# PEER gate matrices with half of the scaled one-hots on GpSimd, and early expert activations in three float32r passes

## The chip, the cores and the metric

The kernel runs on one core of one Trainium2 chip. The metric is the device time of one launch in microseconds (us): the median of the runs shown, which for the kernel before is 4733.09 us (4724.08 to 4733.77, three runs).

The engines are named as the profile names them: PE (TensorE) with its weight loads PEld, DVE (VectorE), ACT (ScalarE), POOL (GpSimd), SP (SyncE, which issues most transfers).

## The reference, cut to what matters

Two layers over 512 latent and 256 context tokens of width 1024. Each layer mixes tokens with four branches and then looks up experts (PEER). The change is in the second part alone, which for each block of 128 tokens computes:

```python
q = (xb @ wq).reshape(PEER_BLOCK, PEER_HEADS, 2, PEER_DQ)
s = jnp.einsum('thpk,hpnk->thpn', q, subkeys)
sv, si = lax.top_k(s, PEER_TOPK)
...
fv, fi = lax.top_k(cand, PEER_TOPK)
e = jnp.take_along_axis(cidx, fi, axis=-1)
gate = jax.nn.softmax(fv, axis=-1)
act = jax.nn.gelu(jnp.einsum('thkd,td->thk', tab_u[e], xb))
return jnp.einsum('thk,thkd->td', gate * act, tab_v[e])
```

With 8 heads and 16 chosen of each, a token has 128 pairs (sub-key i, sub-key j) out of 128 x 128 experts, and a gate for each pair. All arithmetic is float32.

## The kernel before, in words

**Dense and sparse blocks.** Most blocks (four in the first layer, three in the second) don't gather their experts. Their gates are written as a dense matrix over all 128 x 128 experts, and then `dense` runs through every expert. The other blocks gather, with indirect transfers on POOL, while `dense` runs.

**`peer_front`** (L1316) makes the modulated tokens and the best 16 sub-keys of every list. The tokens lie transposed in `u2T`, as a rounded float32r part and a remainder. A product of two such pairs is three passes of PE (`mm3`, L112): high by high, high by low, low by high. The pair is made by `split` (L108): ACT rounds, DVE subtracts. In the kernel before, `modulate` (L361) also keeps the plain float32 tokens of the dense blocks, in `uf` (tile `u2`).

**`chosen`** (L1383) picks, for one block, the 16 best pairs of every head and their gates. Nearly all of it is a chain of small DVE instructions. For a dense block it ends in three PE transposes (L1458) and one DVE copy into `pst` (L1459): rows are slots, columns tokens, with i, j and gate as three planes.

**`build_gates`** (L1461) turns a block's `pst` into the dense matrix, four tokens at a time; I call that a step. A step is one-hot matrices `ohA` (slot x i) and `ohB` (slot x j) for four tokens, `ohB` scaled by the gate, then one PE product per token, `ohA`^T `ohB`. `ohA` is one DVE comparison of 4 x 128 columns (L1472). `ohB` has two ways: unscaled by DVE in the same form and then scaled on ACT token by token (L1478), or for the last `bd` tokens of the four in one DVE instruction per token that compares and scales (L1480). `bd` is 0, 0, 1, 2 for the dense blocks in turn (table `BD`). The products are plain float32, which PE runs as two passes each (L1482). ACT copies the four results into `gsb` (L1483), and SP writes that to DRAM. There are 128 steps in the first layer and 96 in the second. Five buffers each of `ohA` and `ohB` (`OHB`) let DVE run ahead.

**`early_pieces`** (L1490) is filling for PE meanwhile: the activations of 21 sub-keys (first layer) and 26 (second), that `dense` then need not compute. A piece is eight products of 128 x 128 weights `eu` with the tokens (512 columns in the first layer, 384 in the second), in plain float32 from `uf`, then a gelu on ACT and a transfer to DRAM. `ahead` (L251) loads the next piece's weights as far as two buffers go.

**The order.** A scheduler fixes the order of every engine before the launch, by priorities. `layer` (L397) traces 33% (second layer 48%) of the piece products ahead of the gates and the next 67% (52%) spread over the steps, by `UP`; a step's share is held behind the last product of that step and gives way to everything by 3000 in priority:

```python
for n, b in enumerate(dense):
    sT = slots[n % 2]
    self.chosen(l, top, b, tp, sT=sT)
    for _ in self.build_gates(n, sT, G, bp, BD[n], n == nd - 1):
        done += UP[l][1] / steps
        with tc.issue_after(self.last.ins), self.later(3000):
            go_on()
```

So there are two stretches in each layer, which the text calls **the front** (from the end of `peer_front` to the first one-hot product; DVE chooses for the first block, PE runs pieces) and **the gate loop** (first to last one-hot product). `dense` begins after it.

Of the kernel before, what the change touches and what calls it, by code (L numbers as in the profile page):

```python
# [9 lines left out]
F = mybir.dt.float32  # L10
# [9 lines left out]
KC = 8  # L20
# [32 lines left out]
BD = (0, 0, 1, 2)  # L53
# [26 lines left out]
# heads and their width, of the groups whose heads go through the packs  # L80
# [4 lines left out]
def early(l):  # L85
    """the sub-keys whose activations come ahead of the gates: some evenly apart, and the last two"""
    n = EARLY[l] - 2
    return [127 - i * (128 - 256 // EARLY[l]) // n for i in range(n, -1, -1)] + [126]


class Body:
# [28 lines left out]
    def transposes(self, ps, srcs):  # L120
        """the 128 x 128 pieces srcs, transposed side by side into a bank"""
# [50 lines left out]
    def later(self, by):  # L172
        """what is traced here gives way to the next instructions"""
# [77 lines left out]
    def ahead(self, pieces, lead=LOADP):  # L251
        """(tag, buffers, load, run) in turn, matmul by matmul; the loads run ahead as far as the buffers go"""
# [12 lines left out]
    def mod_pieces(self, l, g, p, parts, bufs):  # L265
        """512 columns of the modulation of a layer, their weights in some parts"""
# [32 lines left out]
    def cond_rows(self, conds, p, tmp, **kw):  # L299
        """silu of the first conditions, each on all partitions"""  # L300
# [9 lines left out]
    def mod_columns(self, l, row, p, ms, bufs=3, upto=8):  # L310
        """parts of the modulation column by column on DVE, row: the conditions; a step: 128 columns"""
# [31 lines left out]
    def folded(self, l, which):  # L343
        """columns of the modulation; where the tokens come normalised only, the norm's own factor and shift are in them"""
# [16 lines left out]
    def modulate(self, cols, blocks, h_src, uT, tok=None, pool=None, c0=0, keep=None, ks=range(KC)):  # L361
# [1440 lines left out]
```

## Time and profile before

| what | before |
|---|---|
| median of three runs | 4733.09 us (4724.08 to 4733.77) |
| profiled execution, its span | 4714.6 us (the page gives its span alone; the median is 18.5 us above that) |
| PE, PEld busy | 4504.4 us (96%), 3814.3 us (81%) |
| DVE, ACT busy | 3787.0 us (80%), 2058.5 us (44%) |
| POOL busy | 1086.3 us (23%): 768 indirect transfers |
| chain that ended last | PE 69%, DVE 10%, DMA 8%, issue 6%, ACT 5%, POOL 1% |

How to read it: the shares are means over the whole launch. The two fronts and gate loops together are 518 us of the span, and there the engines are loaded in another way than in `dense`, which is most of the rest. A duration in the profile reaches over the start of the next instruction of the same engine, so the price of one instruction in a row of many is the distance between two starts.

### The profile page before, as it was taken

Reading aid. Unit: us, or ns where it says so; the run is one execution under the profiler, and the core shown is the slowest. Engines: PE = TensorE matmul, PEld = TensorE weight load, DVE = VectorE, ACT = ScalarE, POOL = GpSimd, SP = SyncE. Lnnn points to the kernel's source line nnn. Section 1 sums busy time; section 2 is a strip of 40 time slices with the busy share of each in tenths; the row PEclk is TensorE's granted clock in tenths of the full one; section 3 lists DMA queues with packets and bytes.
Section 4 is the critical chain, followed back from the end, with each engine's and each line's share of the span. In section 5 each row is a group of like instructions: output and inputs, shape, how many; then the busy total and the mean of one; then the engine's idle time right before and its main releaser. Section 6 shows DMA issues by size and latency. Waiting matters only on the chain.

```text
span 4714.6 us, 67359 instructions
## 1 busy us (share of the span) xinstructions
PE 4504.4 (96%) x24113; PEld 3814.3 (81%) x24113; DVE 3787.0 (80%) x7649; ACT 2058.5 (44%) x3956; POOL 1086.3 (23%) x772
## 2 busy tenths in 40 slices
PE   8999999999989999999999798898999999999998
PEld 6978888885668888888888697787877788888887
DVE  7857655899979899999999875866698787777777
ACT  4357654225952222222222354665339633333333
POOL 0000000000006555655556300000000043333341
PEclk9999999999999999999999899999999999999999
DMA  7844332523679999999999676543426798888885
GB/s 278 289 143 124 108 98 88 206 72 119 192 228 346 340 343 332 339 348 348 346 345 342 212 281 190 177 142 98 157 86 185 252 345 299 296 305 309 305 299 195
DMA packets 495791, 1120.38 MB, mean 238 GB/s; under 512 B 43312, under 2 KB 244832, under 8 KB 486368
## 3 DMA queue, kind: packets, MB, share of 16 engines
q1 hardware_dynamic: 384864, 713.38, 44.3%
q0 software_dynamic: 110592, 402.70, 23.7%
q8 instruction: 190, 3.11, 0.3%
q14 instruction: 145, 1.19, 0.1%
HBM read 975.14 MB, written 140.80 MB: 237 GB/s over the span
## 4 chain that ended last, share of the span: by engine, by line
PE 69%; DVE 10%; DMA 8%; issue 6%; ACT 5%; POOL 1%; SPq 0%; POOLq 0%; DVEq 0%; ACTq 0%
PE acc L115 5%; PE acc L117 5%; PE acc L116 5%; PE act L117 4%; PE act L116 4%; PE act L115 4%; PE S L1504 4%; PE mm L117 3%; PE mm L116 3%; PE mm L115 3%; PE mm L1482 3%; DMA gu<-peer_v,pe 3%; PE sg L115 3%; PE sg L116 3%; PE sg L117 3%
## 5 line engine op out<-in xcount | busy, mean ns | idle before, releaser
L1663 POOL DMA_INDIRECT gu<-peer_u,pe x384 | 535.0, 1393 | 3023.1 <-ACT dwh L109 1400.0
L1675 POOL DMA_INDIRECT gu<-peer_v,pe x384 | 551.1, 1435 | 534.4 <-PE acc L117 224.9
L115 PE MATMUL act<-u2T,duh 128*128 128x512 f32 (+1 forms) x1672 | 609.3, 364 | 21.3 <-ACT duh L109 19.2
L117 PE MATMUL act<-u2T,dul 128*128 128x512 f32 (+1 forms) x1672 | 609.3, 364 | 1.4 <-DVE dul L110 1.4
L115 PE MATMUL acc<-dvh,dwh 128*128 128x512 f32 x1536 | 600.2, 391 | 10.5 <-ACT dwh L109 10.3
L116 PE MATMUL act<-u2T,duh 128*128 128x512 f32 (+1 forms) x1672 | 608.4, 364 | 0.0
L116 PE MATMUL acc<-dvl,dwh 128*128 128x512 f32 x1536 | 600.1, 391 | 0.0
L1681 DVE SCALAR_TENSOR_TENSOR gy<-gu,gwt,gy 128x1024 f32<-128x1024 f32 x381 | 488.5, 1282 | 115.2 <-DMA gu<-peer_v,pe 111.9
L1666 DVE SCALAR_TENSOR_TENSOR gu<-gu,px 128x1024 f32<-128x1024 f32 x384 | 462.5, 1220 | 112.1 <-DMA gu<-peer_u,pe 111.4
L117 PE MATMUL acc<-dvh,dwl 128*128 128x512 f32 x1536 | 545.7, 391 | 1.6 <-DVE dwl L110 1.4
L109 ACT ACTIVATE dwh<-dw 128x512 fp32r<-128x512 f32 (+1 forms) x256 | 148.2, 579 | 884.3 <-DVE dw L1551 884.1
L109 ACT ACTIVATE dvh<-dv 128x1024 fp32r<-128x1024 f32 x256 | 263.4, 1052 | 310.4 <-PE rot L117 196.8
L115 PEld LDWEIGHTS act<-u2T,duh 128*128 128x128 f32 x1672 | 315.3, 189 | 60.1 <-ACT duh L109 19.9
L109 ACT ACTIVATE duh<-du 128x1024 fp32r<-128x1024 f32 x209 | 220.8, 1056 | 310.1 <-PE act L116 238.0
L115 PEld LDWEIGHTS acc<-dvh,dwh 128*128 128x128 f32 x1536 | 288.6, 188 | 72.3 <-ACT dwh L109 15.1
L116 PEld LDWEIGHTS act<-u2T,duh 128*128 128x128 f32 x1672 | 315.3, 189 | 37.6
L117 PEld LDWEIGHTS act<-u2T,dul 128*128 128x128 f32 x1672 | 314.9, 188 | 38.1 <-DVE dul L110 2.9
L117 PEld LDWEIGHTS acc<-dvh,dwl 128*128 128x128 f32 x1536 | 288.4, 188 | 64.5 <-DVE dwl L110 4.4
L116 PEld LDWEIGHTS acc<-dvl,dwh 128*128 128x128 f32 x1536 | 288.7, 188 | 57.6
L110 DVE TENSOR_TENSOR dvl<-dv,dvh 128x1024 fp32r<-128x1024 f32 x256 | 308.6, 1218 | 13.4 <-ACT dvh L109 13.4
L1482 PEld LDWEIGHTS mm<-ohB,ohA 128*128 128x128 f32 x1792 | 234.4, 194 | 98.4 <-ACT ohB L1478 48.0
L1504 PE MATMUL S<-u,eu 128*128 128x384 f32 (+1 forms) x752 | 310.7, 537 | 2.0 <-ACT ege L1507 1.2
(386 smaller groups left out, 10684.0 us busy)
## 6 DMA issues: line engine op xcount, KB each, us to landing
dv<-peer_v SPq DMA_DIRECT2D x256, 512.0 KB, 6.4
du<-peer_ut SPq DMA_DIRECT2D x209, 512.0 KB, 6.5
G<-gsb SPq DMA_DIRECT2D x26, 2048.0 KB, 9.2
wmodc<-wmodc SPq DMA_DIRECT2D x84, 512.0 KB, 4.7
gw<-wgb SPq DMA_DIRECT2D x128, 256.0 KB, 2.9
Gt<-G SPq DMA_DIRECT2D x31, 1024.0 KB, 9.7
eu<-peer_ut SPq DMA_DIRECT2D x47, 512.0 KB, 3.9
Gt<-G SPq DMA_DIRECT2D x31, 768.0 KB, 7.0
```

The source lines that it names most:

```text
L109: a = self.nc.scalar.activation(hi, src, AF.Copy)
L110: return a, self.nc.vector.tensor_tensor(lo, src, hi, op=OP.subtract)
L115: mm(out, lh, rh, start=first, stop=False)
L116: mm(out, lh, rl, start=False, stop=False)
L117: self.pe = mm(out, ll, rh, start=False, stop=last)
L1482: self.last = nc.tensor.matmul(ps[:, s % 4, :], A[:, s, :], B[:, s, :], start=True, stop=True)
L1504: nc.tensor.matmul(ps[:, :n], U[:, k, :], uf[:, k, :], start=k == 0, stop=k == KC - 1)
L1663: dma = nc.gpsimd.indirect_dma_start(out=t, out_offset=None, in_=I['peer_u'], in_offset=bass.IndirectOffsetOnAxis(ap=e[:, k:k + 1], axis=0))
L1666: nc.vector.scalar_tensor_tensor(t, t, 1.0, x, op0=OP.mult, op1=OP.mult, accum_out=act[:, k:k + 1])
L1675: dma = nc.gpsimd.indirect_dma_start(out=t, out_offset=None, in_=I['peer_v'], in_offset=bass.IndirectOffsetOnAxis(ap=e[:, k:k + 1], axis=0))
L1681: nc.vector.scalar_tensor_tensor(y, t, w[:, k:k + 1], y, op0=OP.mult, op1=OP.add)
```

## The change

Both edits are in the two stretches just named.

1. In `build_gates` the last two tokens of every four get their scaled `ohB` from POOL, one instruction each (compare, then multiply). For the first two DVE still compares (now 2 x 128 columns) and ACT still scales. The table `BD` and the single-token DVE form are gone.
2. In `early_pieces` the weights are split by ACT and DVE into a float32r pair, two buffers of each, and a product is three passes from `u2T`. The plain tokens `uf` are gone, and `modulate` uses a rotating tile in their place.

Comments are also taken out all over the file; the diff below leaves them out, and a line that was only split differently.

```diff
-BD = (0, 0, 1, 2)
...
-    def modulate(self, cols, blocks, h_src, uT, tok=None, pool=None, c0=0, keep=None, ks=range(KC)):
+    def modulate(self, cols, blocks, h_src, uT, tok=None, pool=None, c0=0, ks=range(KC)):
...
-            u = keep[:, k, c0:c0 + n] if keep is not None else pool.tile([128, 512], F, name="uf", bufs=3 if tok else 2)[:, :n]
+            u = pool.tile([128, 512], F, name="uf", bufs=3 if tok else 2)[:, :n]
...
-                uf = tp.tile([128, KC, nd * 128], F, name="u2", bufs=1)
...
-                fill = [self.early_pieces(l, i, uf, tp) for i in range(EARLY[l])]
+                fill = [self.early_pieces(l, i, uT, nd * 128, tp) for i in range(EARLY[l])]
...
-    def build_gates(self, n, sT, G, p, bd, last):
+    def build_gates(self, n, sT, G, p, last):
...
+        on = GT // 2
...
-                for o, c, k in ((A, 0, GT), (B, 1, GT - bd)):
+                for s in range(on, GT):
+                    t = t0 + q + s
+                    nc.gpsimd.tensor_scalar(B[:, s, :], self.iota, sT[:, 1, t:t + 1], sT[:, 2, t:t + 1], op0=OP.is_equal, op1=OP.mult)
+                for o, c, k in ((A, 0, GT), (B, 1, on)):
                     nc.vector.tensor_tensor(o[:, :k], iota[:, :k], sT[:, c, t0 + q:t0 + q + k, None].to_broadcast([128, k, 128]), op=OP.is_equal)
...
-                        if s < GT - bd:
-                            nc.scalar.activation(B[:, s, :], B[:, s, :], AF.Copy, scale=sT[:, 2, t:t + 1])
-                        else:
-                            nc.vector.tensor_scalar(B[:, s, :], self.iota, sT[:, 1, t:t + 1], sT[:, 2, t:t + 1],
-                                                    op0=OP.is_equal, op1=OP.mult)
+                    if s < on:
+                        nc.scalar.activation(B[:, s, :], B[:, s, :], AF.Copy, scale=sT[:, 2, t:t + 1])
...
-            return U
-
-        def run(U):
+            W = [p.tile([128, KC, 128], R, name="eu" + x, bufs=2) for x in "hl"]
+            self.split(*W, U)
+            return W
+
+        def run(W):
...
-                nc.tensor.matmul(ps[:, :n], U[:, k, :], uf[:, k, :], start=k == 0, stop=k == KC - 1)
+                self.mm3(ps[:, :n], (W[0][:, k, :], W[1][:, k, :]), (uT[0][:, k, :n], uT[1][:, k, :n]), k == 0, k == KC - 1)
```

How the order of the engines moves. First DVE, first layer, in the gate loop of the first block; `ohA` and `ohB` are the one-hots, `tm`, `ij`, `t` and `fi` belong to the choosing for the next blocks. Before:

```order
L1472 TENSOR_TENSOR ohA<-c_iota,pst_10138 128x512
L1472 TENSOR_TENSOR ohB<-c_iota,pst_10138 128x512
L1444 TENSOR_SCALAR tm<-a_12860 128x64
L1406 MAX_INDEX fi<-fv,c_13465 128x8
L1404 MATCH_REPLACE c_13471<-fv,cand 128x112
```

Now, with the remainder `eul` of a split between two one-hots of a step:

```order
L1402 MATCH_REPLACE c_13778<-fv,cand 128x112
L1475 TENSOR_TENSOR ohA<-c_iota,pst_10138 128x512
L109 TENSOR_TENSOR eul<-eu,euh 128x1024
L1475 TENSOR_TENSOR ohB<-c_iota,pst_10138 128x256
L1447 COPY ij_13100<-t_13101 128x64
L1442 TENSOR_SCALAR tm<-a_13091 128x64 x4
```

DVE's second one-hot is half as wide, and the order holds 21 instructions `eul` in the first layer (2 far ahead, 7 in the front, 12 behind it) and 26 in the second (2, 12, 12). In the first layer 51 small instructions of the choosing (37 and 14 value loads) that stood ahead of the first copy to `pst` now stand behind it; in the second layer 14.

Second, ACT, first layer, the gate loop; `ege` is a piece's gelu, which waits for the piece's last product, and `euh` the rounding of the weights of the piece after the next, into the buffer that this piece has read. Now:

```order
L1480 ACTIVATE ohB<-ohB,pst_10138 128x128 x2
L1482 ACTIVATE gsb<-mm 128x4x32x4
L108 ACTIVATE euh<-eu 128x1024
L1507 ACT_TABLE_LOAD
L1507 ACTIVATE ege<-S 128x512
```

Before, that place held `ege` alone, and a step had up to four scalings instead of two. So `euh` is placed just where its buffer comes free, with a whole piece on PE between it and its use.

Third, POOL, the whole of it but its first rows, as one piece of the difference:

```order
-L1663 DMA gu<-peer_u,pe_14713 128x1024 x128
...
+L1473 ISA
+L1473 TENSOR_SCALAR ohB<-c_iota,pst_10138 128x128 x64
+L1473 TENSOR_SCALAR ohB<-c_iota,pst_10139 128x128 x64
...
+L1663 DMA gu<-peer_u,pe_15140 128x1024 x128
...
+L1473 TENSOR_SCALAR ohB<-c_iota,pst_33012 128x128 x64
```

POOL computes only in the gate loops (64 instructions a block, 256 and 192 in all), ahead of each layer's gathers.

## Rows read from the trace of the kernel before

**Rows 1.** The page's first line.

```profile
span 4714.6 us, 67359 instructions
```

**Rows 2.** Busy time by stretch: first layer's front, its loop, then second layer's.

```profile
core 0: us, PE busy (x) PEld busy (x) DVE busy (x) ACT busy (x) POOL busy (x), PEclk, DMA share, GB/s
1071.00:1128.50 57.50, 52.24 (x134) 23.57 (x132) 55.99 (x334) 16.91 (x27) 0.00 (x0) 0.98 0.41 133
1128.50:1364.30 235.80, 226.11 (x1262) 162.59 (x1263) 217.58 (x638) 211.26 (x579) 0.00 (x0) 0.98 0.61 177
3485.00:3543.50 58.50, 57.28 (x185) 34.03 (x184) 56.66 (x329) 19.66 (x38) 0.00 (x0) 1.00 0.40 120
3543.50:3709.70 166.20, 162.03 (x1000) 130.92 (x999) 135.28 (x302) 159.23 (x463) 0.00 (x0) 0.99 0.69 203
```

**Rows 3.** The one-hot products by line: first layer, then second, first and last start.

```profile
L1482 PE MATMUL mm<-ohB,ohA x1024: 272/275/582, 1128.5 to 1364.3; 128*128 128x128 f32 x171
...
L1482 PE MATMUL mm<-ohB,ohA x768: 272/275/513, 3543.5 to 3709.7; 128*128 128x128 f32 x192
```

**Rows 4.** Chain of waits (start, length): ACT, then PE binding, first layer; second layer's pieces.

```profile
1227.87 1.17 ACT ohB L1478 x4
...
1267.69 0.86 PE S L1504 x2
1268.55 0.89 PE mm L1482 x8
...
3577.86 1.29 PE S L1504 x4
```

**Rows 5.** Timeline of DVE: start and length; a step of the fourth block.

```profile
1314.22 0.68 DVE L1472 TENSOR_TENSOR ohA<-c_iota,pst 128x512 f32<-128x512 f32 x1
1314.82 0.41 DVE L1472 TENSOR_TENSOR ohB<-c_iota,pst 128x256 f32<-128x256 f32 x1
1315.16 0.59 DVE L1480 TENSOR_SCALAR ohB<-c_iota,pst 128x128 f32<-128x128 f32 x2
1315.67 0.68 DVE L1472 TENSOR_TENSOR ohA<-c_iota,pst 128x512 f32<-128x512 f32 x1
```

**Rows 6.** Timeline of PE in `dense`: float32r passes, 512 and 384 columns.

```profile
1445.83 0.39 PE L115 MATMUL act<-u2T,duh 128*128 128x512 f32 x1
...
1449.91 0.39 PE L115 MATMUL act<-u2T,duh 128*128 128x512 f32 x1
...
3736.86 0.34 PE L115 MATMUL act<-u2T,duh 128*128 128x384 f32 x1
...
3738.97 0.33 PE L115 MATMUL act<-u2T,duh 128*128 128x384 f32 x1
```

**Rows 7.** By line, ns min/median/max: the split of `dense`, a gathered block's product on DVE.

```profile
L109 ACT ACTIVATE duh<-du x209: 1038/1061/1067, 1376.7 to 4664.5; 128x1024 fp32r<-128x1024 f32 x105
...
L110 DVE TENSOR_TENSOR dul<-du,duh x209: 1205/1218/1299, 1377.8 to 4666.3; 128x1024 fp32r<-128x1024 f32 x105
...
L1666 DVE SCALAR_TENSOR_TENSOR gu<-gu,px x384: 1202/1219/1285, 1405.2 to 4198.2; 128x1024 f32<-128x1024 f32 x192
```

**Rows 8.** Timeline at the ends of the fronts: first layer, then second.

```profile
1125.38 0.57 DVE L1459 COPY pst<-mm 128x384 f32<-128x384 f32 x1
...
1128.48 2.08 PE L1482 MATMUL mm<-ohB,ohA 128*128 128x128 f32 x8 [5.26 <-ACT ohB L1478]
...
3533.73 9.94 PE L1504 MATMUL S<-u,eu 128*128 128x384 f32 x30 [1.22 <-ACT ege L1507]
...
3537.72 0.57 DVE L1459 COPY pst<-mm 128x384 f32<-128x384 f32 x1
```

**Rows 9.** Groups of the first gate stretch (busy, mean ns), and one gather on POOL.

```profile
L1478 ACT ACTIVATE ohB<-ohB,pst 128x128 f32<-128x128 f32 x416 | 135.2, 405 | 12.7 <-DVE ohB L1472 12.6
L1480 DVE TENSOR_SCALAR ohB<-c_iota,pst 128x128 f32<-128x128 f32 x96 | 29.9, 339 | 0.0
...
1402.26 0.94 POOL L1663 DMA_INDIRECT gu<-peer_u,pe  x1 [0.30 <-issue]
```

More of the change, by code (lines that the diff above doesn't have):

```diff
@@ L443, in layer @@
                 slots = [tp.tile([128, 4, 128], F, name=f"pst{i}", bufs=1) for i in range(2)]
-                uf = tp.tile([128, KC, nd * 128], F, name="u2", bufs=1)
-                top = self.peer_front(l, blocks, dense, sparse, uT, uf, kp, tp, hp)
+                top = self.peer_front(l, blocks, dense, sparse, uT, kp, tp, hp)
                 self.ge = self.dram.tile([EARLY[l], 128, nd * 128], F, name=f"ge{l}")
                 bp = self.pool(s2, "pb", 2)
-                fill = [self.early_pieces(l, i, uf, tp) for i in range(EARLY[l])]
+                fill = [self.early_pieces(l, i, uT, nd * 128, tp) for i in range(EARLY[l])]
                 if need:
@@ L468, in layer @@
                     self.chosen(l, top, b, tp, sT=sT)
-                    for _ in self.build_gates(n, sT, G, bp, BD[n], n == nd - 1):
+                    for _ in self.build_gates(n, sT, G, bp, n == nd - 1):
                         done += UP[l][1] / steps
@@ L1313, in outproj, with peer_front @@
             pass
-    def peer_front(self, l, blocks, dense, sparse, uT, uf, kp, tp, hp):
+    def peer_front(self, l, blocks, dense, sparse, uT, kp, tp, hp):
         nc, I = self.nc, self.I
@@ L1340, in peer_front @@
                     u, c0 = (uC, 0) if b == LB else (uT, 128 * b)
-                    self.modulate(cols, blocks[b:b + w], self.z, u, self.x2, tmp, c0, uf if b < len(dense) else None)
+                    self.modulate(cols, blocks[b:b + w], self.z, u, self.x2, tmp, c0)
             hp.release()
@@ L1470, in build_gates @@
                 B = p.tile([128, GT, 128], F, name="ohB", bufs=OHB)
-                for o, c, k in ((A, 0, GT), (B, 1, GT - bd)):
+                for s in range(on, GT):
+                    t = t0 + q + s
+                    nc.gpsimd.tensor_scalar(B[:, s, :], self.iota, sT[:, 1, t:t + 1], sT[:, 2, t:t + 1], op0=OP.is_equal, op1=OP.mult)
+                for o, c, k in ((A, 0, GT), (B, 1, on)):
                     nc.vector.tensor_tensor(o[:, :k], iota[:, :k], sT[:, c, t0 + q:t0 + q + k, None].to_broadcast([128, k, 128]), op=OP.is_equal)
-                for q4 in range(0, GT, 4):
-                    ps = self.ps.tile([128, 4, 128], F, name="mm")
-                    for s in range(q4, q4 + 4):
-                        t = t0 + q + s
-                        if s < GT - bd:
-                            nc.scalar.activation(B[:, s, :], B[:, s, :], AF.Copy, scale=sT[:, 2, t:t + 1])
-                        else:
-                            nc.vector.tensor_scalar(B[:, s, :], self.iota, sT[:, 1, t:t + 1], sT[:, 2, t:t + 1],
-                                                    op0=OP.is_equal, op1=OP.mult)
-                        self.last = nc.tensor.matmul(ps[:, s % 4, :], A[:, s, :], B[:, s, :], start=True, stop=True)
-                    nc.scalar.activation(gs[:, :, q + q4:q + q4 + 4, :].rearrange("p b t j -> p t b j"),
-                                         ps.rearrange("p t (b j) -> p t b j", j=JB), AF.Copy)
+                ps = self.ps.tile([128, GT, 128], F, name="mm")
+                for s in range(GT):
+                    t = t0 + q + s
+                    if s < on:
+                        nc.scalar.activation(B[:, s, :], B[:, s, :], AF.Copy, scale=sT[:, 2, t:t + 1])
+                    self.last = nc.tensor.matmul(ps[:, s, :], A[:, s, :], B[:, s, :], start=True, stop=True)
+                nc.scalar.activation(gs[:, :, q:q + GT, :].rearrange("p b t j -> p t b j"),
+                                     ps.rearrange("p t (b j) -> p t b j", j=JB), AF.Copy)
                 yield
@@ L1488, in build_gates, with early_pieces @@
                 nc.sync.dma_start(G[a:z, :, n * 128 + t0:n * 128 + t0 + TG, :].rearrange("b i t j -> i b t j"), gs[:, a:z])
-    def early_pieces(self, l, i, uf, p):
+    def early_pieces(self, l, i, uT, n, p):
         nc = self.nc
         j = early(l)[i]
-        n = uf.shape[2]
         def load():
```

## The prediction

> **What bounds the kernel now.** I read the busy time by stretch first, because the change lives in two stretches of each layer and the shares of the whole launch say little about them. The gate loop runs from the first to the last one-hot product: 1128.5 to 1364.3 in the first layer, 3543.5 to 3709.7 in the second [rows 3], so 236 and 166 us. In the first loop three engines are nearly full at once: PE 226, DVE 218 and ACT 211 of 236 us. In the second PE has 162 and ACT 159 of 166, DVE 135 [rows 2]. The reader should see that relieving one engine alone gains little, and that POOL has nothing to do there. The chain of waits then shows a step where PE binds: 0.89 us of one-hot products and 0.86 us for a piece's product, one behind the other with no gap [rows 4].
>
> The fronts differ. In the first layer DVE is busy for 56.0 of 57.5 us [rows 2], and PE stands idle for 5.26 us before the first one-hot product, which comes 3 us after the copy to `pst` [rows 8]: the choosing on DVE sets the end. In the second the copy is done at 3538.3, yet PE works on pieces until 3543.5 [rows 8]: PE sets it, with DVE some 5 us ahead.
>
> **Prices, part by part.** *Pieces on PE.* A plain float32 product takes 0.86 us at 512 columns and 1.29 / 2 = 0.645 us at 384 [rows 4]. A float32r pass starts every (1449.91 - 1445.83) / 18 = 0.227 us at 512 columns and (3738.97 - 3736.86) / 12 = 0.176 us at 384, 18 and 12 being the passes between [rows 6]. Three passes cost 0.68 and 0.53 us, so a product gains 0.18 and 0.12 us. The loops hold 109 and 114 such products (the passes counted in the trace, halved): PE gains 20 us in the first, 13 us in the second.
>
> *One-hots on DVE.* Starts lie 0.60 us apart behind 512 columns, 0.34 behind 256, and 0.51 / 2 = 0.255 behind a compare-and-scale of one token [rows 5]; for 384 columns I take the middle, 0.47. A step now costs 0.60 + 0.60 = 1.20 us in blocks with `bd` 0, 0.60 + 0.47 + 0.26 = 1.33 with 1, 0.60 + 0.34 + 0.51 = 1.45 with 2. With 64, 32 and 32 steps that is 77 + 43 + 46 = 166 us in the first loop; with 64 and 32, 77 + 43 = 120 us in the second. The new step is 0.60 + 0.34 = 0.94 us: 120 and 90 us. DVE gains 46 and 30 us.
>
> *Splits.* The rounding costs ACT 1.06 us and the remainder costs DVE 1.22 us [rows 7]. By the order 12 of each lie in either loop: 13 us on ACT, 15 us on DVE. ACT loses 160 scalings in each loop (416 less 256, 352 less 192); at 1.17 / 4 = 0.29 us, where the chain runs through four of them [rows 4], that is 47 us. So ACT is down by 34 us in both and can't bind.
>
> *Fronts.* In the first layer 7 splits, 8.5 us, enter ahead of the copy to `pst`, and the order moves 51 small instructions behind it, which at the front's mean of 56.0 / 334 = 0.17 us [rows 2] are 8.6 us. The front keeps its length; the loop's DVE gets the 8.6 us. PE is done with its pieces earlier and only waits longer. In the second layer 12 splits, 14.6 us, enter and 14 instructions, 2.4 us, leave. The copy then comes 12 us later, less the 1.8 us that DVE idles there now [rows 2]: 3548, and the first one-hot product 3 us behind, 3551 instead of 3543.5. **The second front loses 8 us**, although PE has less to do.
>
> *The rest of the loops, without POOL.* DVE in the first: 218 - 166 + 120 + 15 + 9 = 195 us; in the second 135 - 120 + 90 + 15 + 2 = 123 us. PE: 226 - 20 = 206, and 162 - 13 = 149 us. With the slack that PE has now (10 and 4 us) the loops would take 216 and 153 us.
>
> *POOL.* It gets 256 and 192 instructions of a kind that no row shows on it. The nearest rows are the same compare-and-scale on DVE (0.255 us apart, mean length 0.339) and the scaling alone on ACT (mean 0.405); the far end is POOL's own gather, 0.94 us [rows 5, 9]. I take 0.34 us, the length of the very same instruction, and 0.255 to 0.405 as bounds: 87 us (65 to 104) in the first loop, 65 us (49 to 78) in the second. Either way POOL alone is far from binding.
>
> *POOL beside DVE.* What matters is whether POOL's 87 us lie beside DVE's 195 or in turn with them. The lower bound is no cost: a DVE product with two inputs keeps its median of 1219 ns and never exceeds 1285 over all 384 times, while gathers are issued on POOL [rows 7]. The upper bound is full turns, 195 + 87 = 282 us. The row for the lower bound is of an engine that issues transfers; the new instruction streams 128 columns of `iota` from the memory DVE reads, so I give that row little weight and take turns as the likelier. For its price I go between two counts: turns with one-hots and splits alone, 120 + 15 + 87 = 222 us, everything else of DVE beside; and turns with all of DVE, 282. The middle is 252. In the second loop 90 + 15 + 65 = 170 to 123 + 65 = 188, middle 179.
>
> Here the Trainium skill speaks against the change. "SBUF — State Buffer", section "SBUF: two separate sides", says that GpSimd shares one pair of ports with VectorE, that a VectorE instruction with two SBUF inputs and a GpSimd instruction that reads SBUF exclude each other for their whole length, and that the loser waits. The row on gathers shows no such thing, and no run here has GpSimd computing. By the row the sum is 4708, by the rule it is the forecast.
>
> **The sum.** First loop 252 - 236 = +16, second 179 - 166 = +13, second front +8: +37 us. The sum is made on an execution with a span of 4714.6 us [rows 1], 18.5 below the median; I add it to the median: 4733 + 37 = **4770 us**. With 0.255 us the loops are 230 and 163 (middles): -6 - 3 + 8, 4732. With 0.405 they are 269 and 192: +33 + 26 + 8, 4800; and with 0.405 and full turns 299 and 201: +63 + 35 + 8, 4839.
>
> "GPSIMD Engine Reference", section "Elementwise — side-by-side cycle accounting", gives 769 ns for 512 elements in its best case, an estimate of 0.19 us for 128; no row here shows it. By that price turns would cost so little that PE binds again, and the sum would be 4708.
>
> **The rivals.**
> *POOL beside DVE (faster).* If the two don't exclude each other, PE binds: 216 - 236 = -20, 153 - 166 = -13, +8: -25 us, **4708**. It speaks for it that DVE keeps its pace beside gathers; against it, that DVE is full in the first loop and any loss there shows at once. It decides at a POOL price below about 0.2 us in turns, or at any price below 0.8 us beside (206 / 256).
>
> *The gains cancel (same).* With turns at the low price the sum is 4732. Late splits would do the same to the rival above: each piece's remainder must wait for the last product of the piece two before, then for ACT and for DVE's queue. The order places `euh` where its buffer comes free, a whole piece ahead of its use; eight products with their steps last some 14 us in the loop against 1.06 + 1.22. So I don't expect PE to wait for them. If it did by 1 us in each of 24, 4708 would become 4732.
>
> *POOL alone binds (slower).* At the gather's 0.94 us the loops would be 241 and 180 us even beside DVE: +5 + 14 + 8, 4760. Both ends at once, 0.94 in turns, would be 4733 + 300; I leave that out, since the nearest rows are the same arithmetic.
>
> That the change does not do what it says I exclude: the order shows 64 POOL instructions in each block's place and 21 and 26 splits.
>
> **How the numbers follow.** About 0.2%, 9.5 us, can be told from no change. Turns at 0.34 us or near: 0.48, slower. POOL alone binding: 0.07, slower. Beside, or so short that turns don't matter: 0.33, faster. Cancelled: 0.12, same. So faster 0.33, same 0.12, slower 0.55. The likeliest case's own range is 4745 to 4840. Eight times in ten must reach to the faster case as well: from 4698 (its 4708 without the 10 us of slack that PE has in the first loop) to 4840.
>
> **What would show it.** Right: POOL's instructions stretch where DVE compares, DVE's one-hots lie further apart than 0.60 and 0.34 us or wait, both loops last 250 and 180 us, PE's clock and idle time there get worse, ACT has time to spare, and the second front ends near 3551. Each step alone: product triples at 0.68 and 0.53 us, DVE's remainders at 1.22 us, ACT below 180 us in the first loop. Wrong: loops of 216 and 153 us with PE without gaps (beside), POOL rows in an unbroken line (POOL alone), or PE waiting for `eul` at the start of each piece.

## The result and the profile after

The changed kernel takes **4873.44 us** (median of four runs, 4862.36 to 4879.57); the kernel before, in the four runs beside and before it, takes 4728.59 us. The ratio is 1.0315, with a 95% interval of 1.0302 to 1.0328: slower by 145 us. I had forecast 4770 us, slower, and had given 4840 us as the far end of the range.

The profiled execution of the changed kernel has a span of 4870.1 us, against 4714.6 [rows 1], so 155.5 us are to be found. The table of busy time by stretch, with the columns of [rows 2], for the first front, the first gate loop, the second front and the second loop:

```profile
1078.30:1135.90 57.60, 42.24 (x188) 33.98 (x186) 56.62 (x301) 22.53 (x32) 2.90 (x3) 0.89 0.40 133
1135.90:1437.10 301.20, 242.43 (x1376) 195.56 (x1376) 207.93 (x595) 186.83 (x432) 300.29 (x254) 0.96 0.46 135
3565.60:3633.60 68.00, 56.11 (x313) 54.55 (x311) 65.43 (x324) 29.14 (x43) 2.95 (x3) 0.94 0.40 128
3633.60:3855.00 221.40, 178.62 (x1094) 161.65 (x1095) 133.86 (x302) 139.51 (x321) 221.16 (x190) 0.93 0.48 140
```

The loops last 301.2 and 221.4 us instead of 235.8 and 166.2 [rows 3]: +65.4 and +55.2 us. The reader should look at POOL: it is busy for 300.3 of 301.2 us and for 221.2 of 221.4, while no other engine is full. From the first piece product to the first one-hot product, the first front keeps its 57 us and the second goes from 58.8 to 68.0, +9.2. The modulation ahead of the fronts (first transposition of `z` to first product of the queries) goes from 21.3 to 25.7 us and from 16.1 to 18.6, +4.4 and +2.5. Together that is 137 of the 155.5 us. The rest lies in stretches that the edit does not touch, 10 us of it behind the second loop (from its last one-hot product to the end 1015.1 us against 1004.9, where the runs below show 999 to 1020); the profiled execution of before happens to lie 14 us below the median of its runs, that of after 3 us.

The end of the second front in the timeline, where the copy stood at 3537.72 [rows 8] and the first one-hot product at 3543.5 [rows 3]: the copy comes 92.2 us later than before, 80.9 of it brought along from the stretches ahead of the front, and the first one-hot product now follows the copy by 3.6 us, so that DVE sets the end:

```profile
3629.92 0.56 DVE L1457 COPY pst<-mm 128x384 f32<-128x384 f32 x1
```

```profile
3633.56 2.08 PE L1481 MATMUL mm<-ohB,ohA 128*128 128x128 f32 x8 [5.51 <-ACT ohB L1480]
```

Who waits for whom shows in the view of the line of the one-hot products (durations: minimum, median, maximum in ns; then the idle time of PE and PEld ahead of them, in us and times; then who waited for them):

```profile
L1481 PE MATMUL mm<-ohB,ohA x1792: 270/275/582, 1135.9 to 3855.0; 128*128 128x128 f32 x200
...
  POOL ohB L1473: 229.9, 323
  ACT ohB L1480: 35.1, 27
...
  ACT gsb L1482: 157.8, 166
  DVE ohA L1475: 147.4, 159
```

PE and its weight loads wait for POOL's one-hots, and DVE and ACT wait in turn for PE. The 229.9 us are a sum of two engines that mostly wait side by side: POOL's line, below, has 95.6 us for PE and 134.3 for the weight loads. Behind it stands the line of DVE's compares, after and then before:

```profile
L1473 POOL TENSOR_SCALAR ohB<-c_iota,pst x448: 787/1094/5538, 1133.0 to 3854.0; 128x128 f32<-128x128 f32 x150
...
  PEld mm L1481: 134.3, 173
  PE mm L1481: 95.6, 150
```

```profile
L1475 DVE TENSOR_TENSOR ohA<-c_iota,pst x224: 660/693/864, 1134.4 to 3846.2; 128x512 f32<-128x512 f32 x112
```

```profile
L1472 DVE TENSOR_TENSOR ohA<-c_iota,pst x224: 628/682/762, 1126.6 to 3704.5; 128x512 f32<-128x512 f32 x112
```

One step in the timeline (start and length in us; the last row of POOL is two instructions) puts the two side by side:

```profile
1391.13 0.69 DVE L1475 TENSOR_TENSOR ohA<-c_iota,pst 128x512 f32<-128x512 f32 x1 [1.16 <-PE mm L1481]
1391.31 1.43 POOL L1473 TENSOR_SCALAR ohB<-c_iota,pst 128x128 f32<-128x128 f32 x1
1391.73 0.42 DVE L1475 TENSOR_TENSOR ohB<-c_iota,pst 128x256 f32<-128x256 f32 x1
1392.72 2.21 POOL L1473 TENSOR_SCALAR ohB<-c_iota,pst 128x128 f32<-128x128 f32 x2
1392.79 0.49 PE L1481 MATMUL mm<-ohB,ohA 128*128 128x128 f32 x2 [0.33 <-POOL ohB L1473]
1393.32 0.69 DVE L1475 TENSOR_TENSOR ohA<-c_iota,pst 128x512 f32<-128x512 f32 x1 [1.16 <-PE mm L1481]
```

A step takes 1393.32 - 1391.13 = 2.19 us. DVE compares for 1.03 us of it at the pace it had before, and then idles for 1.16. POOL does one instruction in 1.41 us (1392.72 - 1391.31), beside DVE's compares, and one in 0.78, while DVE idles; then it starts again, without a gap.

Over all steps this is regular. Between POOL instructions that stand back to back the distance of two starts is never below 0.774 us. Where DVE's instructions with two input tiles (the compares, the remainders, and in the choosing the predicated copies) fill under a quarter of that distance, its mean is 0.78 us (168 times); where they fill half to three quarters, 1.28 (134 times); above that, 1.65 (127 times). A straight line through all of them is 0.68 us + 0.63 x (time of DVE's two-input instructions beside it) + 0.10 x (time of DVE's other instructions), which explains 87% of the variance. These times are the recorded lengths, which overlap; cut at the next start, the same fit gives 0.77 instead of 0.63, so 0.63 goes with recorded lengths alone. The mean is 1.179 us, and 256 x 1.179 = 302 us is the first loop.

So there were two theories to try. *Price and turns*: POOL's instruction costs 0.775 us by itself, DVE's two-input work lengthens it to 1.18, POOL alone pays, and POOL thereby binds. *The rest of the change*: splits, remainders and the rotating tile stretch the loops, and POOL only fills the time.

### The profile page after: what moved, and what is told of

The parts are those of the page before. It is cut to its first block, busy times and chain, and to the rows that moved or that the text cites. A ratio compares the mean times of both kernels' runs of the same rounds, so it can differ in the third digit from the quotient of the medians.

```text
span 4870.1 us, 68681 instructions
## 1 busy us (share of the span) xinstructions
PE 4528.4 (93%) x24489; PEld 3911.2 (80%) x24489; DVE 3788.7 (78%) x7568; ACT 2034.9 (42%) x3685; POOL 1611.0 (33%) x1220
## 5 line engine op out<-in xcount | busy, mean ns | idle before, releaser
L1473 POOL TENSOR_SCALAR ohB<-c_iota,pst 128x128 f32<-128x128 f32 x448 | 527.3, 1191 | 2038.7 <-DVE pst L1457 2038.7
L1481 PE MATMUL mm<-ohB,ohA 128*128 128x128 f32 x1792 | 304.1, 300 | 112.5 <-POOL ohB L1473 95.6
L1481 PEld LDWEIGHTS mm<-ohB,ohA 128*128 128x128 f32 x1792 | 260.8, 201 | 171.0 <-POOL ohB L1473 134.3
L116 PEld LDWEIGHTS acc<-dvh,dwl 128*128 128x128 f32 x1536 | 288.6, 188 | 67.8 <-DVE dwl L109 7.7
```

The lines of the kernel that those rows point to most:

```text
L116: self.pe = mm(out, ll, rh, start=False, stop=last)
L1473: nc.gpsimd.tensor_scalar(B[:, s, :], self.iota, sT[:, 1, t:t + 1], sT[:, 2, t:t + 1], op0=OP.is_equal, op1=OP.mult)
L1481: self.last = nc.tensor.matmul(ps[:, s, :], A[:, s, :], B[:, s, :], start=True, stop=True)
```

## The experiments

Loop times are from first to last one-hot product of each run's profile; the ratio is to the kernel before, run beside it on the same chip (medians of 4720 to 4729 us), with its 95% interval. Three kernels were run once and have no interval.

| run | first, second loop | time, us | ratio |
|---|---|---|---|
| before | 235.8, 166.2 | 4728.59 | |
| changed | 301.2, 221.4 | 4873.44 | 1.0315 [1.0302, 1.0328] |
| split pieces alone | 247.0, 173.9 | 4762.64 | 1.0084 [1.0069, 1.0100] |
| POOL half alone | 288.6, 213.2 | 4816.95 | 1.0196 [1.0179, 1.0212] |
| one of four on POOL | 248.1, 169.8 | 4755.92 | 1.0065 [1.0049, 1.0081] |
| one of four, plain pieces | 232.0, 159.5 | 4719.25 | 0.9998 [0.9987, 1.0008] |
| no compares on DVE | 239.9, 165.2 | 4734.77 | one run |
| DVE compares token by token | 269.8, 188.3 | 4794.27 | 1.0147 [1.0122, 1.0172] |
| half of the columns on POOL | 299.5, 211.3 | 4856.08 | one run |
| compare alone on POOL | 255.0, 179.3 | 4775.89 | one run |
| split alone, 8 rotating tiles | 245.9, 172.9 | 4751.51 | 1.0059 [1.0043, 1.0076] |
| remainders on POOL | 251.8, 179.2 | 4778.91 | 1.0125 [1.0108, 1.0141] |
| shared | 251.3, 177.4 | 4774.12 | 1.0111 [1.0092, 1.0130] |
| extra POOL instruction | 249.6, 178.1 | 4772.70 | 1.0110 [1.0093, 1.0127] |

### The two halves of the change

**Split pieces alone**: the changed kernel with `build_gates` and `BD` of before.

```diff
-    for _ in self.build_gates(n, sT, G, bp, n == nd - 1):
+    for _ in self.build_gates(n, sT, G, bp, BD[n], n == nd - 1):
```

> The split pieces alone, the one-hots as before. If POOL's one-hots make the whole loss of the loops (+65 and +55 us), it goes away here: the loops come back to about 240 us (DVE: its 218 of before, 15 of remainders, 9 of work moved out of the front) and 172 us (ACT 159 + 13), no PE wait for a one-hot of over 20 us in all; with the second front's +9 and the rotating tile's +7 the time is 4740 to 4770 us. If the splits or the three passes are what stretches the loops, they stay above 260 and 190 us and the time above 4800.

The loops came out at 247.0 and 173.9 us. The windows of the two loops, columns as in [rows 2]:

```profile
1137.50:1384.50 247.00, 222.37 (x1376) 190.14 (x1376) 239.26 (x691) 224.37 (x592) 0.00 (x0) 0.96 0.56 165
3577.40:3751.30 173.90, 161.04 (x1096) 154.28 (x1096) 154.05 (x334) 172.82 (x481) 0.00 (x0) 0.95 0.61 179
```

DVE binds the first (239 us, 242 by my prices) and ACT the second (173 us, 172 by my prices). The splits are thus a loss of their own, +11 and +8 us in the loops, but not the 65 and 55. The time, 4763, lies in the range that I gave. That PE's waits for a one-hot would be small was wrong: PE and its weight loads together waited 114.2 us for `ohB` as ACT scaled it (PE alone 47.9), where they waited 66.1 (PE 18.1) in the kernel before.

**POOL half alone**: the kernel before with the new `build_gates`.

> Half of the scaled one-hots on POOL alone, the early pieces in plain float32. If POOL binds the loops by itself: PE waits for POOL's one-hots again, by over 150 us in all, the loops are 280 to 300 and 205 to 220 us, the fronts and the modulation are those of before, and the time is 4820 to 4850 us. If the splits on DVE are needed for the loss (DVE too full, POOL shut out by the remainders), the loops are below 260 and 185 us and the time is below 4780.

Loops of 288.6 and 213.2 us, fronts of 56.6 and 58.8 as before; the time, 4817, is 3 us below what I expected. The line of the one-hot products says why (waits of PE and PEld added, as above; PE alone has 60.4):

```profile
  POOL ohB L1475: 161.6, 325
```

POOL's mean distance is 1.128 us here, and 256 x 1.128 = 289. Without the remainders DVE has less two-input work, and POOL is a little shorter: the turns, in small. Against the 4724.25 us of the kernel before in these runs the two halves cost 38 and 93 us, 131 together; both at once cost 145.

### What POOL's instruction costs, and what lengthens it

**No compares on DVE** but one for each block, which leaves most of the first one-hots out of the computation.

```diff
+        A = p.tile([128, GT, 128], F, name="ohA", bufs=1)
+        nc.vector.tensor_tensor(A, iota, sT[:, 0, 0:GT, None].to_broadcast([128, GT, 128]), op=OP.is_equal)
...
-                A = p.tile([128, GT, 128], F, name="ohA", bufs=OHB)
...
-                for o, c, k in ((A, 0, GT), (B, 1, on)):
-                    nc.vector.tensor_tensor(o[:, :k], iota[:, :k], sT[:, c, t0 + q:t0 + q + k, None].to_broadcast([128, k, 128]), op=OP.is_equal)
...
-                        nc.scalar.activation(B[:, s, :], B[:, s, :], AF.Copy, scale=sT[:, 2, t:t + 1])
+                        nc.scalar.activation(B[:, s, :], A[:, s, :], AF.Copy, scale=sT[:, 2, t:t + 1])
```

> DVE's compares of two inputs are taken out of the loop: one product of 128x512 a block, which all its tokens then use as their first one-hot and as the source of the half that ACT scales. This leaves part of the computation out; POOL, PE and ACT issue what they did. If DVE's two-input work is what lengthens POOL's instructions, POOL's rows fall to 0.78 to 0.82 us in the mean and the loops to 205 to 220 and 150 to 160 us (PE binds), time 4715 to 4750 us. If POOL's 1.19 us is its own price beside any busy engine (PE and ACT reading the same memory), the rows stay above 1.1 us and the loops at 290 and 210 us or more.

```profile
L1474 POOL TENSOR_SCALAR ohB<-c_iota,pst x448: 782/788/2381, 1133.0 to 3730.3; 128x128 f32<-128x128 f32 x150
```

The median falls from 1094 to 788 ns, the mean distance to 0.881 us, and the loops to 239.9 and 165.2 us. PE, ACT and the pieces were as busy as before beside it, so it was DVE's work that lengthened POOL's. The mean and the loops miss what I expected (0.82 us and 220, 160). For the mean the reason shows: the remainders and the choosing of the next block are still on DVE, and beside them the distances are 0.88 to 1.24 us. For the first loop it explains a part only: POOL is busy for 224.7 and PE for 221.0 of its 239.9 us, so neither fills it.

**DVE's compares token by token**, with one input tile and a scalar each; ACT scales nothing.

```diff
-                for o, c, k in ((A, 0, GT), (B, 1, on)):
-                    nc.vector.tensor_tensor(o[:, :k], iota[:, :k], sT[:, c, t0 + q:t0 + q + k, None].to_broadcast([128, k, 128]), op=OP.is_equal)
+                for s in range(GT):
+                    t = t0 + q + s
+                    nc.vector.tensor_scalar(A[:, s, :], self.iota, sT[:, 0, t:t + 1], None, op0=OP.is_equal)
+                for s in range(on):
+                    t = t0 + q + s
+                    nc.vector.tensor_scalar(B[:, s, :], self.iota, sT[:, 1, t:t + 1], sT[:, 2, t:t + 1], op0=OP.is_equal, op1=OP.mult)
```

> DVE's six one-hots a step one token at a time, each from one tile and the token's own scalar, instead of two products of two tiles; ACT scales nothing. If only DVE's two-input instructions hold POOL up, POOL's rows fall to 0.78 to 0.90 us; DVE then binds with 6 x 0.255 = 1.53 us a step where it had 0.94: 195 + 75 = 270 us in the first loop and 123 + 57 = 180 in the second, loops 270 to 280 and 180 to 192 us, time 4800 to 4825 us. If any DVE instruction that reads this memory holds POOL up, POOL's rows stay at 1.2 us or above and the loops are 300 and 220 us or longer, time above 4860.

```profile
L1473 POOL TENSOR_SCALAR ohB<-c_iota,pst x448: 783/906/2387, 1130.3 to 3784.2; 128x128 f32<-128x128 f32 x150
```

DVE issues more instructions and is busier (253 of 269.8 us against 208 of 301), and yet POOL's median is 906 ns instead of 1094, and the whole is 79 us faster than the changed kernel. The loops, 269.8 and 188.3 us, have the length that I expected of DVE, and the time is 6 us below; but POOL fills the first as much as DVE does (256 us against 253), and PE and its weight loads wait longer for POOL:

```profile
  POOL ohB L1473: 107.9, 220
  DVE ohB L1479: 25.8, 12
```

So it is not how busy DVE is that lengthens POOL's instructions. What differs is the form of the compares, two input tiles or one; they also became shorter (0.28 us instead of 0.69 at the median), and no run here separates the two.

**Half of the columns.** POOL makes 64 of the 128 columns of its one-hots, DVE the others.

```diff
-                    nc.gpsimd.tensor_scalar(B[:, s, :], self.iota, sT[:, 1, t:t + 1], sT[:, 2, t:t + 1], op0=OP.is_equal, op1=OP.mult)
+                    for e, c in ((nc.gpsimd, 0), (nc.vector, 64)):
+                        e.tensor_scalar(B[:, s, c:c + 64], self.iota[:, c:c + 64], sT[:, 1, t:t + 1], sT[:, 2, t:t + 1],
+                                        op0=OP.is_equal, op1=OP.mult)
```

> POOL makes 64 of the 128 columns of each of its one-hots, DVE the other 64, one token at a time. If POOL's price goes by columns, its shortest start-to-start falls from 0.775 to about 0.39 us; if it is mostly a fixed cost, it stays above 0.6 us. DVE gets 256 more instructions of some 0.2 us, so 195 + 51 = 246 us in the first loop and 123 + 38 = 161 in the second: loops about 250 and 170 us in the first case, 270 or more and 195 or more in the second.

```profile
L1474 POOL TENSOR_SCALAR ohB<-c_iota,pst x448: 570/1200/3216, 1128.8 to 3833.3; 128x64 f32<-128x64 f32 x150
```

The shortest distance is 0.553 us against 0.774: between the two cases. By these two points a fixed 0.33 us and 3.5 ns a column. The median, though, is 1200 ns, longer than for the whole width, and the loops are 299.5 and 211.3 us: DVE got 256 instructions more and is busy for 257 us of the first. What the cheaper POOL instruction gave, the added work of DVE took: POOL is busy for 272 us of that loop, no longer for all of it.

**Compare alone**, without the gate (`op1` and its scalar left out):

> POOL compares and does not multiply by the gate: this leaves the gates of half of the tokens out. If POOL's price is that of its two operations, the shortest start-to-start falls from 0.775 us to 0.5 us or less and the loops to 250 to 270 and 180 to 195 us; if the price is that of streaming 128 columns, whatever is done with them, it stays at 0.70 to 0.78 us and the loops at 295 to 302 and 215 to 222 us.

```profile
L1473 POOL TENSOR_SCALAR ohB<-c_iota,pst x448: 597/1047/4192, 1129.4 to 3761.1; 128x128 f32<-128x128 f32 x150
```

The shortest distance is 0.578 us, so the multiplication costs 0.196 of the 0.774; the loops are 255.0 and 179.3 us. Both operations count, beside a part that is paid once. Here DVE's compares stand beside POOL as in the changed kernel, and a cheaper POOL instruction gives 46 and 42 us back: so POOL's price binds the loops.

### Fewer one-hots on POOL

**One of four**, with split pieces, and **one of four with plain float32 pieces**: `on = 3 * GT // 4` in the changed kernel, and in the run of POOL half alone.

> As changed, but one scaled one-hot of four on POOL instead of two. If POOL's time per instruction (0.78 us alone, 1.2 us beside DVE's compares) is the bound, one a step is 1.2 us against PE's 206 / 128 = 1.6 us a step, and POOL no longer binds: loops 220 to 235 and 155 to 165 us, PE's wait for POOL under 30 us in all, time 4725 to 4745 us. If each POOL instruction takes its time away from DVE whatever their number, DVE has 212 us of its own plus 128 x 0.8 in the first loop and the loops stay at 270 and 190 us or more: time above 4790.

> One scaled one-hot of four on POOL, and the early pieces in plain float32 as before: no splits, no rotating tile, no second front. PE binds with its 226 and 162 us. If POOL's own time is the bound of the change, this is where it costs nothing and DVE and ACT get slack: loops 228 to 234 and 162 to 166 us, time 4715 to 4729 us. If POOL's instructions slow DVE or PE in some other way, the loops are longer than those of before, 245 and 172 or more, and the time is above 4740.

The windows of the loops, first the two with split pieces, then the two with plain ones:

```profile
1134.30:1382.40 248.10, 218.47 (x1369) 190.96 (x1370) 217.38 (x594) 214.92 (x560) 223.61 (x127) 0.94 0.56 164
3583.90:3753.70 169.80, 155.13 (x1094) 149.88 (x1095) 143.38 (x302) 156.45 (x417) 156.95 (x95) 0.96 0.62 183
```

```profile
1127.10:1359.10 232.00, 219.68 (x1255) 162.21 (x1255) 196.55 (x542) 201.71 (x547) 198.75 (x127) 0.97 0.61 180
3540.60:3700.10 159.50, 155.75 (x985) 127.03 (x984) 122.15 (x270) 143.27 (x398) 140.82 (x93) 1.00 0.70 207
```

With split pieces every load is near the one worked out (DVE 217 against 212 us, ACT 215), but the first loop is 248 us, not 220 to 235, and the time 11 us above what I expected: four engines with 215 to 224 us of work each do not run full at once. I read that as a ring of engines that feed one another, which no run tests by itself. POOL alone, with half the instructions, is busy for 224 us; its mean distance is now 1.70 us where instructions stand back to back, I take it because DVE's compares leave it fewer gaps. With plain pieces PE binds again and the loops gain 4 and 7 us. The time is that of the kernel before within the interval: of the gain 6 us are lost behind the second loop (1010.5 us to the end, against 1004.9), inside the scatter of that stretch.

### The smaller terms

**Eight rotating tiles** in the split-only kernel:

```diff
-            u = pool.tile([128, 512], F, name="uf", bufs=3 if tok else 2)[:, :n]
+            u = pool.tile([128, 512], F, name="uf", bufs=8 if tok else 2)[:, :n]
```

> The split pieces alone (the one-hots as before), with eight buffers of the rotating tile of the modulation instead of three. If the three buffers are what lengthens the modulation (23.9 against 19.5 us in the first layer, 18.9 against 16.1 in the second, from the first transposition to the first product of the queries), it comes back to 19.5 and 16.1 and the time falls by 7 us against the split pieces alone: 4750 to 4760 us. If the longer modulation has another cause, both stretches stay and the time is 4758 to 4768 us.

The time fell into the first theory's range, yet its mechanism did not show: from the first transposition of `z` to the first product of the queries it is still 26.7 us in the first layer and 18.6 in the second. (Up to the last transposition, where the expectation's 23.9 and 19.5 us of the first layer end, it is 24.8 us.) The buffers are not the cause. Nor do they make the 11 us in the median (the intervals overlap): between the two profiled executions 5.4 us of it lie ahead of the first modulation and 5.5 between the first loop and the second modulation, where the edit touches nothing. The timeline of DVE in the changed kernel's second modulation shows what else is new there:

```profile
3453.27 1.23 DVE L109 TENSOR_TENSOR eul<-eu,euh 128x1024 fp32r<-128x1024 f32 x1 [1.42 <-ACT euh L108]
3454.41 0.40 DVE L377 TENSOR_SCALAR uf<-mm,fold 128x128 f32<-128x128 f32 x1
3454.73 1.22 DVE L109 TENSOR_TENSOR eul<-eu,euh 128x1024 fp32r<-128x1024 f32 x1
```

The splits of the first two pieces are placed into each layer's modulation: remainders of 2.45 us on DVE, which waits 1.42 us for ACT's rounding ahead of the first. As lengths the remainders match the 2.5 us of the second layer, and leave about 2 of the first layer's 4.4 open. That they alone are the cause is not shown: in the next run, with the remainders on POOL, the second modulation still takes 17.4 us, and DVE there waits 2.21 us for ACT, which rounds the same two pieces.

**Remainders on POOL**, one-hots as before (with the eight tiles), and **shared**: the same, and one one-hot of four on POOL in the first two blocks.

```diff
-            self.split(*W, U)
+            nc.scalar.activation(W[0], U, AF.Copy)
+            nc.gpsimd.tensor_tensor(W[1], U, W[0], op=OP.subtract)
```

> As the last, and the remainders of the split pieces are computed on POOL instead of DVE; no one-hot on POOL. With the price that the runs so far give (0.33 us and 3.5 ns a column) a remainder of 1024 columns takes 3.9 us undisturbed and 4 to 8 us beside DVE's compares, a piece ahead of its use. If POOL pays for the turns and DVE does not: DVE has 227 us in the first loop, ACT 224, loops 228 to 236 and 172 to 176 us (ACT binds the second), the second front is back at 59 to 61 us, time 4722 to 4740 us. If the remainders take longer than a piece (over 8 us), PE waits for them, in the second front first: front above 68 us, time above 4760.

> As the last, and in the first two blocks of a layer one scaled one-hot of four on POOL. ACT falls to 205 us in the first loop and 153 in the second, DVE to 219 and 128, PE has 206 and 149, POOL 64 x 1.7 + 12 x 6 = 180 us at most. If only POOL's own load counts, nothing binds but PE and DVE: loops 218 to 226 and 153 to 160 us, time 4700 to 4715 us, faster than both kernels. If POOL's remainders and one-hots hold each other up in POOL's queue, PE waits for ohB from POOL by over 20 us and the time is 4730 or more.

Both missed, by 39 and 59 us; the second front, 70.2 and 69.0 us, got no shorter either. The time and the front are those named for remainders that come too late for PE, but PE waited only 1.4 us for them. DVE lost its remainders, and still its busy time in the first loop rose, from 239.4 us (eight tiles) to 243.5. The timeline of DVE and of POOL in the first run shows where it went:

```profile
1148.52 2.86 POOL L1499 TENSOR_TENSOR eul<-eu,euh 128x1024 fp32r<-128x1024 f32 x1 [26.14 <-PE S L116]
```

```profile
1148.50 0.68 DVE L1471 TENSOR_TENSOR ohB<-c_iota,pst 128x512 f32<-128x512 f32 x1
1149.10 2.83 DVE L1471 TENSOR_TENSOR ohA<-c_iota,pst 128x512 f32<-128x512 f32 x1
1151.85 0.68 DVE L1471 TENSOR_TENSOR ohB<-c_iota,pst 128x512 f32<-128x512 f32 x1
```

POOL's instruction waits out the compare that runs (2.86 us instead of 2.34 at the shortest), and the next compare then waits for all of POOL's. Here DVE pays, some 2 us for each remainder, more than the 1.22 that was taken off it. DVE's compare-and-scale, which has one input tile, waits in the same way, as its longest shows:

```profile
L1479 DVE TENSOR_SCALAR ohB<-c_iota,pst x128: 327/336/2470, 1275.1 to 3761.4; 128x128 f32<-128x128 f32 x128
```

Beside the remainders DVE's instructions are longer than their medians in the run with eight tiles by 1.8 us in the mean in the first loop, and by about 15 us in all in the second front, as much as was taken off DVE there. The shared version, whose ACT load fell to 207 us as worked out, ends at 251 us with DVE at 241.6; there PE and its weight loads also waited 34.7 us for POOL's one-hots (PE alone 16.4), where over 20 was named as the sign of a queue on POOL, so that a queue may have its part in it.

**An extra POOL instruction** of one input tile and 1024 columns for each piece, in the split-only kernel, whose result nobody reads:

```diff
             self.split(*W, U)
+            X = p.tile([128, KC * 128], F, name="eux", bufs=1)
+            nc.gpsimd.tensor_scalar(X, U.rearrange("p k c -> p (k c)"), self.iota[:, 0:1], self.iota[:, 1:2], op0=OP.is_equal, op1=OP.mult)
```

> The split pieces alone (remainders on DVE, one-hots as before), and one more POOL instruction for each piece whose result nobody reads: a compare and multiply over the 1024 columns of the loaded weights, one tile in and two scalars. Undisturbed it should last 0.33 + 1024 x 0.0035 = 3.9 us. In the run with remainders on POOL, DVE's instructions waited up to 2.4 us beside a POOL instruction of two tiles and 2.3 us length. If it was the two tiles that made DVE wait, DVE beside the new instruction keeps 0.68 us for a product and 0.34 for a compare-and-scale, the loops stay at 245 to 250 and 172 to 176 us and the time at 4748 to 4768 us; the POOL instruction is the one that stretches. If it was the length of the POOL instruction, DVE's instructions last up to 4 us here and the loops are 270 and 195 us or more, time above 4800.

```profile
L1500 POOL TENSOR_SCALAR eux<-eu,c_iota x47: 3780/4229/12191, 908.1 to 3729.3; 128x1024 f32<-128x1024 f32 x47
```

```profile
L1471 DVE TENSOR_TENSOR ohA<-c_iota,pst x224: 630/679/1444, 1133.5 to 3757.3; 128x512 f32<-128x512 f32 x112
```

The shortest is 3.78 us, where the fixed part and the columns gave 3.9. Neither theory holds whole: DVE's median stays at 679 ns, but next to many of these instructions one instruction of DVE takes 0.7 us longer (a compare 1.44 instead of 0.68 us), and then DVE goes on while POOL still runs. So DVE does not wait for the length of a one-input instruction on POOL; it waits for a part of it, mostly once, and POOL's instruction stretches as well, to 12.19 us at the longest. The loops, 249.6 and 178.1 us, are 3 and 4 us longer than in split pieces alone, and the time is 5 us above the range of the first theory.

## Why the prediction was wrong, and where it held

*The step that failed* is POOL's price: "I take 0.34 us, the length of the very same instruction, and 0.255 to 0.405 as bounds", together with "Both ends at once, 0.94 in turns, would be 4733 + 300; I leave that out, since the nearest rows are the same arithmetic". The same arithmetic on another engine was no near row. Undisturbed, the instruction takes 0.774 us, over twice the value taken and close to the gather's 0.94 that I put aside. That 0.94 was one row and no far end either: the page of before has these gathers at 1.39 us in the mean.

*Turns* were real, but sized and booked wrongly. I added DVE's and POOL's time in the first loop, between one-hots and splits alone and all of DVE. With 0.774 us that sum would be 135 + 198 = 333 to 195 + 198 = 393 us; the loop was 301, because POOL gives up 0.63 us for each us of DVE's two-input work and hardly anything for the rest. A price too low and turns too full partly cancelled: 252 forecast, 301 measured; 179 and 221 in the second loop.

*Who pays* was wrong as well. I wrote that DVE's one-hots would lie further apart. They keep their pace (693 ns against 682 at the median), POOL's stretch, PE waits for POOL, and DVE for PE. The rival "POOL alone binds" (0.07) named the wait, at a price without turns; what came is that wait with the price of the turns in it.

*What held.* By the view of the line of the splits from 1000 to 1500 us, and by the timeline of PE in the first front:

```profile
L109 DVE TENSOR_TENSOR eul<-eu,euh x19: 1175/1219/1265, 1090.4 to 1380.5; 128x1024 fp32r<-128x1024 f32 x19
```

```profile
1085.06 0.39 PE L114 MATMUL S<-u2T,euh 128*128 128x512 f32 x1
...
1086.42 0.39 PE L114 MATMUL S<-u2T,euh 128*128 128x512 f32 x1
```

Passes in the fronts start (1086.42 - 1085.06) / 6 = 0.227 and, in the second layer, 0.173 us apart, as taken from `dense`; between one-hot products a triple takes 0.78 us instead of 0.68, but the one-hot product ahead of it, in the run of split pieces alone, 0.08 less, net 0.70 (in the second loop 0.61 instead of 0.53, net 0.53). ACT's and DVE's splits have the lengths taken (DVE's median 1219 ns). The split's loads on DVE and ACT came within 3 us in the run that did it alone. The second front loses 9.2 us where I had 8, and the first keeps its length. PE's granted clock in the loops went from 0.98 and 0.99 to 0.96 and 0.93, with the idle time, as named. *What was left out*: two splits of each layer fall into the modulation, with 2.45 us of remainders, and a rotating tile that I did not price turned out to cost nothing measurable. ACT in the first loop was busy for 186.8 us, where I had named less than 180 as a sign, and DVE for 207.9, where the sum had 195. For DVE most of that is counting: a step's two compares now stand alone and count 1.02 us where I had priced 0.94.

*The rule that I weighed.* The Trainium skill, "SBUF — State Buffer", section "SBUF: two separate sides", has DVE's two-input instructions and GpSimd's exclude each other, the first to start keeping the ports for its whole length. The run with remainders on POOL shows just that, 2.83 us instead of 0.68. There DVE's compare-and-scale, with one input tile, waited too, 2.47 us instead of 0.34. For GpSimd's instructions with one input the traces show less: POOL loses 0.63 us a us, and a compare of DVE beside an instruction of 3.8 us or more at most 0.77 us (1.444 against 0.679).

The other page of the Trainium skill that I cited, "GPSIMD Engine Reference", section "Elementwise — side-by-side cycle accounting", gave an estimate of 0.19 us; the measured 0.774 us decides. The same section's measured addition of two tiles, 4497 ns at 2048 columns, gives an estimate of 2.25 us at 1024, and here the trace agrees: POOL's remainder takes 2.34 us at the shortest.

*What stays open.* No version beat the kernel before by more than its interval. The one that came nearest, one of four on POOL with plain pieces, suggests why: PE fills 226 and 162 us of the loops of before, so relieving DVE and ACT frees little, and the pieces that relieve PE cost DVE more than it has.

## What to carry to other kernels

Before work goes to an idle engine, price the instruction on that engine, at its own shape and with its own scalars; where no row shows it there, its length on another engine is no bound, and the far end of the range belongs into the forecast. Then ask what runs beside it: where POOL computes next to DVE's compares of two tiles, count for POOL its own price and, by the fit of this case, 0.63 us for every recorded us of them, and where POOL's instruction itself has two input tiles, count its whole length as a possible stall of DVE. Last, where three engines are near full in a stretch, a relief of one, or a load on a fourth, has to be worked out against all of them: one of four with split pieces took 248 us with the fullest engine at 224.

## What was not expected of the hardware

- POOL's compare-and-scale of 128 columns takes 0.774 us undisturbed: by the runs of 64 and 128 columns some 0.33 us fixed and 3.5 ns a column, which gave 3.9 us for 1024 columns where 3.78 were measured. Without the multiplication it is 0.578 us.
- A subtraction of two tiles of 1024 columns takes POOL 2.34 us, less than a compare-and-scale of one tile of that width with two scalars, 3.78.
- A row of DVE compares can keep POOL out for long. Once, in the run with remainders on POOL, one of them took 8.89 us: ten compares and a predicated copy followed one another on DVE, and only a later copy waited for POOL. It is no rule: in the two timelines of that run shown above, POOL got in between two compares of such a row.

```profile
1204.82 8.89 POOL L1499 TENSOR_TENSOR eul<-eu,euh 128x1024 fp32r<-128x1024 f32 x1 [15.22 <-ACT euh L1498]
```

```profile
1204.77 0.67 DVE L1471 TENSOR_TENSOR ohA<-c_iota,pst 128x512 f32<-128x512 f32 x1
...
1210.17 0.69 DVE L1471 TENSOR_TENSOR ohB<-c_iota,pst 128x512 f32<-128x512 f32 x1
1210.78 0.73 DVE L1444 COPY_PREDICATED t<-tm,sif 128x512 f32<-128x512 uint32 x1
...
1211.89 2.41 DVE L1444 COPY_PREDICATED t<-tm,sif 128x512 f32<-128x512 uint32 x1
```
